# One fixed TensorE order for the attention of a two-layer hybrid block

## The chip, the cores and the metric

One core of a Trainium2 chip runs the whole program. The metric is device time in microseconds (us) of one execution, the median over runs. TensorE multiplies, VectorE (DVE), ScalarE (ACT) and GpSimd (POOL) do the elementwise work, and SyncE (SP) starts most DMAs.

## The reference

Two consecutive layers work on 512 latent tokens and 256 context tokens of width 1024. Layer 0 (a recurrent RWKV mixer with pooling, then a SwiGLU FFN) is not touched by the change. Layer 1 is neighbourhood attention over an 8 x 64 grid with 16 heads of 64, where every query also sees all 256 context keys in the same softmax, and then a SwiGLU FFN. The part that changes, cut to its core:

```python
q, k, v = split(h @ w_in, 3)                 # 512 latent tokens
kc, vc  = split(hc @ w_in[:, D:], 2)         # 256 context tokens
# each grid query looks at an 8 x 16 window, with a learned 2-D relative bias
s_loc = einsum('bqhd,bqnhd->bhqn', qr, kg) * scale + bias
s_ctx = einsum('bqhd,bnhd->bhqn', qr, kc) * scale
p = softmax(concatenate([s_loc, s_ctx], -1))
o = einsum('bhqn,bqnhd->bqhd', p[..., :n_loc], vg) + einsum('bhqn,bnhd->bqhd', p[..., n_loc:], vc)
out_lat = o.reshape(B, L, D) @ w_out
```

## The kernel before, in words

Activations lie with the 1024 features on partitions, as 8 slices of 128 features by 512 tokens. Every float32 product of activations with weights is made of three products of split operands (`mm3`, lines 115 to 121): high x high, high x low, low x high. A weight tile comes in by a DMA from the SP queue (`fetch`, lines 825 to 831), ACT casts its high part and DVE subtracts to get its low part.

Attention runs head pair by head pair: slice m of 8 holds heads 2m and 2m+1, one on partitions 0 to 63, the other on 64 to 127. For each m:

- `queries` (lines 644 to 658) makes the pair's q and k: two columns of 8 `mm3` each, so 2 x 24 matmuls of 512 columns, each column in a PSUM bank of tag `w` (two banks). After a column, ACT writes the high part (line 657 or 654) and DVE the low part (line 658 or 655).
- `attention` (lines 660 to 720) first loads the bias of both heads (4 DMAs from the SP queue, 6 POOL additions, line 675). Then it goes through 4 blocks `cb` of 128 queries. In each, for head j = 0 and then 1: six score matmuls of 256 columns with 64 rows (lines 686 and 687, recorded as lines 119 to 121) into a bank of tag `y` (three banks); the softmax (DVE lines 689, 693, 696; ACT line 695 with its accumulator read; POOL line 697); four transposes of 128 columns (line 700) into a bank of tag `v` (two banks) and ACT's copy of them (line 702). When both heads are there, 8 products with the values (line 711, recorded as 16 matmuls, the two heads on the two column halves) go to tag `s`, and every second block ACT copies them out (line 716, or 719 and 720 for the last pair).
- `mixed` (lines 722 to 728) casts the outputs of the first seven slices for the output projection `mixer_out` (8 columns of 8 `mm3`, 192 matmuls of 512 columns).

`latents` (lines 763 to 771) computes the values and the queries of pair 0, then for each m emits `attention(m)` together with `queries(m + 1)`, and for the last m with `mixed`. What order the engines run is not the order of emission: a planner takes, for each engine, among the instructions that its own model holds to be ready the one with the highest priority, which is the emission order here. So score, query, transpose and value matmuls of one or two pairs lie mixed on TensorE. `tc.issue_after(x)` is the one means to fix an order: what is emitted under it goes behind x in the queue of its engine.

Of the kernel before, what the change touches and what calls it, by code (L numbers as in the profile page):

```python
# [9 lines left out]
F32 = mybir.dt.float32  # L10
F32R = mybir.dt.float32r
AF = mybir.ActivationFunctionType
ALU = mybir.AluOpType
AX = mybir.AxisListType
PSUM = bass.MemoryType.PSUM

P = 128
# [12 lines left out]
CWR_, CWL_ = 3, 3  # L30
LATL, KEYL = 9, 0
REST = 1
POOL_S = 0
LEV = dict(c=1, C=2, p=0, s=0, q=1, m=4, a=5, l=5, L=5, X=2)

# [2 lines left out]
KD = 8  # L38
TL, TC = 512, 256
# [27 lines left out]
def chained(*gens):  # L67
    for g in gens:
        yield from g


class Kernel:
    def __init__(self, ctx, tc, a, out):
        self.ctx, self.tc, self.nc, self.a, self.out = ctx, tc, tc.nc, a, out
        self.now = 0
        self.ps = {}
        self.const = ctx.enter_context(tc.tile_pool(name="const", bufs=1))
        self.wp = ctx.enter_context(tc.tile_pool(name="wp", bufs=2))
# [36 lines left out]
    def mm3(self, ps, l, r, first, last, after=None):  # L115
        (lh, ll), (rh, rl) = l, r
        mm = self.nc.tensor.matmul
        with self.tc.issue_after(after.ins) if after else nullcontext():
            mm(ps, lhsT=lh, rhs=rh, start=first, stop=False)  # L119
        mm(ps, lhsT=lh, rhs=rl, start=False, stop=False)  # L120
        self.last = mm(ps, lhsT=ll, rhs=rh, start=False, stop=last)  # L121


    def setup(self):
# [519 lines left out]
    def queries(self, ap, f, m):  # L644

        nc, a = self.nc, self.a
        V = nc.vector
        new = lambda nm, n: [ap.tile([P, n], F32R, name=nm + s, tag=nm + s, bufs=2) for s in ("hi", "lo")]
        q, k = self.qk[m] = new("q", TL), new("k", TL)
        for j, src in enumerate((a.wq, a.wk)):  # L650
            ps = self.bank("w", (TL,))
            yield from f.column(ps, src[m], KD, f.act)
            if j:
                nc.scalar.copy(out=k[0], in_=ps)
                V.tensor_tensor(out=k[1], in0=ps, in1=k[0], op=ALU.subtract)
            else:
                nc.scalar.mul(out=q[0], in_=ps, mul=0.125)
                V.scalar_tensor_tensor(out=q[1], in0=ps, scalar=0.125, in1=q[0], op0=ALU.mult, op1=ALU.subtract)

    def attention(self, ap, f, m, o):  # L660
        nc, a = self.nc, self.a
        V, mm = nc.vector, nc.tensor.matmul
        v, vs = self.v
        (q, k), kc, vc = self.qk[m], self.kc[m], self.vc
        bm = []
        for j in range(2):

            run = ap.tile([P, 272], F32, name="run", tag="run", bufs=2)
            for hf in range(2):
                off = 16 + (2 * m + j) * 480 + 8 * hf  # L670
                src = bass.AP(a.rpb.tensor, a.rpb.offset + off, [[32, 8], [1, 8], [1, 272]])
                nc.sync.dma_start(out=run[64 * hf:64 * hf + 64, :], in_=src)
            b = ap.tile([P, 3, 256], F32, name="bm", tag="bm", bufs=3)
            for ty in range(3):
                nc.gpsimd.tensor_tensor(out=b[:, ty], in0=run[:, 8 * ty:8 * ty + 256], in1=self.mask[:, ty], op=ALU.add)
            bm.append(b)
        po = self.bank("s", (4, P))
        for cb in range(4):
            ty = (0, 1, 1, 2)[cb]
            gs = (0, 1, 3, 4)[cb]  # L680
            sT = [None] * 2
            for j in range(2):
                hd = slice(64 * j, 64 * j + 64)
                ps = self.bank("y")
                lq = tuple(x[hd, cb * P:cb * P + P] for x in q)
                self.mm3(ps[:, 0:256], lq, tuple(x[hd, 64 * gs:64 * gs + 256] for x in k), True, True)
                self.mm3(ps[:, 256:512], lq, tuple(x[hd, :] for x in kc), True, True)
                loc = ps[:, 0:256].rearrange("p (g r c) -> p g r c", g=4, r=8)
                V.tensor_tensor(
                    out=loc, in0=loc, in1=bm[j][:, ty, ::-1].rearrange("p (r g c) -> p g r c", g=4, r=8), op=ALU.add  # L690
                )
                mx = ap.tile([P, 2], F32, name="mx", tag="mx", bufs=4)
                V.tensor_reduce(out=mx[:, 0:1], in_=ps, axis=AX.X, op=ALU.max, negate=True)
                s = f.tmp("s")
                nc.scalar.activation(out=s, in_=ps, func=AF.Exp, bias=mx[:, 0:1], accum_out=mx[:, 1:2])
                V.reciprocal(out=mx[:, 1:2], in_=mx[:, 1:2])
                nc.gpsimd.tensor_scalar(out=s, in0=s, scalar1=mx[:, 1:2], scalar2=0.0, op0=ALU.mult, op1=ALU.add)
                pt = self.bank("v", (4, P))
                for i in range(4):
                    nc.tensor.transpose(out=pt[:, i, :], in_=s[:, i * P:i * P + P], identity=self.ident)  # L700
                sT[j] = f.tmp("sT", "ln").rearrange("p (i t) -> p i t", i=4)
                nc.scalar.copy(out=sT[j], in_=pt)
                yield 1
            for i in range(4):
                for j in range(2):
                    if i < 2:
                        src = v[:, gs // 2 + i] if gs % 2 == 0 else vs[:, gs // 2 + i]
                    else:
                        src = vc[:, i - 2]
                    hc = slice((2 * m + j) * 64, (2 * m + j) * 64 + 64)  # L710
                    mm(po[64 * j:64 * j + 64, cb, :], lhsT=src[:, hc], rhs=sT[j][:, i, :], start=i == 0, stop=i == 3)  # L711
            if cb % 2:
                cs = slice(P * cb - P, P * cb + P)
                done = po[:, cb - 1:cb + 1].rearrange("p c t -> p (c t)")
                if m < KD - 1:
                    nc.scalar.copy(out=o[:, m, cs], in_=done)
                else:
                    hi, lo = f.act(m)
                    nc.scalar.copy(out=hi[:, cs], in_=done)  # L719
                    V.tensor_tensor(out=lo[:, cs], in0=done, in1=hi[:, cs], op=ALU.subtract)  # L720

    def mixed(self, f, o):

# [6 lines left out]
    def latents(self, right):  # L730

        nc, a, tc, ctx = self.nc, self.a, self.tc, self.ctx
        self.turn = 0
        pool = lambda st, name, side="left": st.enter_context(tc.tile_pool(name=name, bufs=1, side=side))
        kv = pool(ctx, "kv")
        psl = self.psum("psl", "y")
        self.banks["y"] = 3
        ctx.enter_context(psl)
        f = Flow(self, pool(ctx, "lp"), "l", TC, TL, 0, "ywywy", LBG, dict(t=3, ln=4, f=2, whi=3, wlo=3))
        f.load()  # L740
        f.mix()
        run = lambda g: [None for _ in g]
        with self.level(LATL):
            run(f.mixer_out(0, a.w_out, MIX))
        with ExitStack() as st:
            gp = pool(st, "gp")
            new = lambda: gp.tile([P, 512], F32, name="aw", tag="aw", bufs=NAW_)
            md = lambda: gp.tile([P, 512], F32, name="md", tag="aw", bufs=NAW_)
            self.emit((LATL, f.ffn(0, gp, 4, 5), 528), (LATL, self.adas([(1, g) for g in range(12)], lambda: self.bank("v"), new, NAW_, md), 150))
            last = self.last  # L750
            self.join_norm(1)
            self.join_norm(2)
            with self.level(KEYL):
                run(self.context_keys(kv, last))
            run(f.normed(1))
        right.close()
        with ExitStack() as st:
            ap = pool(st, "ap")
            self.mask = ap.tile([P, 3, 256], F32, name="mask")
            nc.scalar.dma_start(out=self.mask, in_=a.mask)  # L760
            self.qk = [None] * KD
            o = ap.tile([P, KD, TL], F32, name="o")
            run(self.values(ap, f))
            run(self.queries(ap, f, 0))
            for m in range(KD):
                parts = [(0, self.attention(ap, f, m, o), 8)]
                if m + 1 < KD:
                    parts.append((0, self.queries(ap, f, m + 1), 16))
                else:
                    parts.append((0, self.mixed(f, o), 7))  # L770
                self.emit(*parts)
        run(f.mixer_out(2, a.w_out1))
        run(f.ffn(1, pool(ctx, "gp1"), 11, 16))
        run(f.normed(3, True))
# [666 lines left out]
```

## Time and profile before

| | before |
|---|---|
| median of 3 runs | 2420.7 us (2420.57 to 2421.53) |
| profiled execution, device time | 2430.38 us |
| its span, first to last instruction | 2428.6 us |
| TensorE busy | 2212.5 us (91%) |
| VectorE busy | 1220.3 us (50%) |
| ScalarE busy | 996.7 us (41%) |
| GpSimd busy | 659.6 us (27%) |

The profile is one execution, recorded on the chip. A row of the timeline gives the start of an instruction, how long it took, its engine, its source line, the operation, and "out<-in" with the program's tile names. Matmuls overlap: the distance between the starts of two neighbours is what a matmul costs TensorE, not its own duration. All `mm3` matmuls bear lines 119 to 121; in the attention those with 64 rows are scores, those with tiles `lhhi`, `lhlo`, `whi`, `wlo` are the projections.

### The profile page before, as it was taken

How to read it: one execution, taken by the hardware profiler on the slowest of the kernel's cores; microseconds unless marked ns; L12 is line 12 of the kernel's file. 1: busy time of each engine (PE TensorE's matmuls, PEld its weight loads, DVE VectorE, ACT ScalarE, POOL GpSimd, SP SyncE). 2: the span in 40 equal slices, each digit the busy share in tenths (PEclk: the TensorE clock that was granted, in tenths of full speed). 3: DMA queues.
4: the chain of work that ended last, by engine and by line, in shares of the span. 5: the costliest groups of instructions: out<-in, count | busy, mean ns of one | idle time of the engine just before them, and what ended most of it. 6: DMA issues, size and time to landing. Idle time of an engine off the chain costs nothing.

```text
span 2428.6 us, 44519 instructions
## 1 busy us (share of the span) xinstructions
PE 2212.5 (91%) x16944; PEld 1760.6 (72%) x16944; DVE 1220.3 (50%) x2529; ACT 996.7 (41%) x2075; POOL 659.6 (27%) x643
## 2 busy tenths in 40 slices
PE   7888888889879898979999999998999998999995
PEld 4776666656657777758788877877777776888874
DVE  2756555636656764225633553357454465333343
ACT  3545334444534643334533332234354544322332
POOL 2431202121322432556732300023133342000021
PEclk9888889879978899989999999999999998999997
DMA  7765466566843454575544335323511112333332
GB/s 268 230 181 176 116 193 185 169 173 183 235 125 91 137 141 121 160 252 185 174 127 130 115 124 165 99 83 113 144 45 49 43 52 66 96 95 97 96 90 66
DMA packets 324678, 327.35 MB, mean 135 GB/s; under 512 B 137328, under 2 KB 214768, under 8 KB 324464
## 3 DMA queue, kind: packets, MB, share of 16 engines
q1 hardware_dynamic: 320720, 317.45, 44.1%
q10 hardware_dynamic: 2592, 3.90, 0.5%
q8 instruction: 133, 2.18, 0.4%
q0 software_dynamic: 1152, 3.15, 0.3%
q14 instruction: 81, 0.66, 0.1%
HBM read 280.02 MB, written 42.80 MB: 133 GB/s over the span
## 4 chain that ended last, share of the span: by engine, by line
PE 62%; DVE 6%; DMA 5%; ACT 2%; issue 1%; SPq 1%; POOL 0%; POOLq 0%; DVEq 0%; ACTq 0%
PE y L119 8%; PE y L120 7%; PE y L121 7%; PE w L119 6%; PE w L121 6%; PE w L120 6%; PE s L119 3%; PE s L120 3%; PE s L121 3%; PE s L711 2%; PE v L700 1%; PE v L195 1%; PE w L1099 1%; DVE n L879 1%; DVE pr L1133 1%
## 5 line engine op out<-in xcount | busy, mean ns | idle before, releaser
L829 ACT CAST whi<-wraw 128x512 fp32r<-128x512 f32 (+2 forms) x560 | 329.3, 593 | 697.8 <-PE y L120 261.1
L830 DVE TENSOR_TENSOR wlo<-wraw,whi 128x512 fp32r<-128x512 f32 (+2 forms) x384 | 285.7, 747 | 357.2 <-ACT whi L829 330.3
L830 POOL TENSOR_TENSOR wlo<-wraw,whi 128x512 fp32r<-128x512 f32 (+2 forms) x176 | 202.4, 1157 | 297.2 <-ACT whi L829 269.7
L107 POOL TENSOR_TENSOR wlo<-wraw,whi 128x512 fp32r<-128x512 f32 x92 | 121.5, 1322 | 290.0 <-ACT whi L106 260.8
L119 PE MATMUL w<-lhhi,whi 128*128 128x512 f32 x472 | 189.2, 402 | 9.9 <-ACT lhhi L954 5.3
L119 PE MATMUL y<-lhhi,whi 128*128 128x512 f32 x488 | 192.3, 394 | 0.5 <-ACT lhhi L719 0.5
L121 PE MATMUL y<-lhhi,wlo 128*128 128x512 f32 x488 | 190.5, 391 | 0.0
L120 PE MATMUL y<-lhlo,whi 128*128 128x512 f32 x488 | 190.5, 390 | 0.0
L120 PE MATMUL w<-lhlo,whi 128*128 128x512 f32 x472 | 188.1, 399 | 1.8 <-DVE lhlo L879 1.5
L121 PE MATMUL w<-lhhi,wlo 128*128 128x512 f32 x472 | 187.4, 397 | 0.1
L855 POOL TENSOR_TENSOR lxz<-lxz,s 128x512 f32<-128x512 f32 x28 | 43.3, 1579 | 510.3 <-ACT s L861 510.3
L119 PE MATMUL s<-chhi,whi 128*128 128x256 f32 x480 | 144.5, 301 | 23.0 <-DVE kclo L610 9.3
L119 PE MATMUL g<-hhi,whi 128*128 128x256 f32 (+1 forms) x368 | 140.4, 381 | 14.2 <-DVE nr L480 5.4
L121 PE MATMUL s<-chhi,wlo 128*128 128x256 f32 x480 | 142.4, 297 | 0.4 <-POOL wlo L830 0.4
L120 PE MATMUL s<-chlo,whi 128*128 128x256 f32 x480 | 142.8, 297 | 0.0
L121 PE MATMUL g<-hhi,wlo 128*128 128x256 f32 (+1 forms) x368 | 137.1, 373 | 2.0 <-POOL wlo L107 1.8
L120 PE MATMUL g<-hlo,whi 128*128 128x256 f32 (+1 forms) x368 | 134.1, 364 | 0.0
L119 PEld LDWEIGHTS s<-chhi,whi 128*128 128x128 f32 x480 | 96.5, 201 | 31.4 <-DVE kclo L610 9.7
L119 PEld LDWEIGHTS w<-lhhi,whi 128*128 128x128 f32 x472 | 89.1, 189 | 33.6 <-ACT lhhi L926 7.5
L119 PEld LDWEIGHTS y<-lhhi,whi 128*128 128x128 f32 x488 | 91.9, 188 | 21.9 <-issue 3.0
L120 PEld LDWEIGHTS w<-lhlo,whi 128*128 128x128 f32 x472 | 89.4, 189 | 25.3 <-DVE lhlo L879 4.9
L121 PEld LDWEIGHTS y<-lhhi,wlo 128*128 128x128 f32 x488 | 91.8, 188 | 19.6 <-DVE n L879 0.8
(360 smaller groups left out, 5138.6 us busy)
## 6 DMA issues: line engine op xcount, KB each, us to landing
wraw<-w SPq DMA_DIRECT2D x368, 256.0 KB
aw<-ada_w SPq DMA_DIRECT2D x128, 256.0 KB
wraw<-w_in SPq DMA_DIRECT2D x92, 256.0 KB
bk<-bk SPq DMA_DIRECT2D x72, 256.0 KB
wraw<-ada_w SPq DMA_DIRECT2D x64, 256.0 KB
wraw<-w_out SPq DMA_DIRECT2D x48, 256.0 KB
wraw<-wk SPq DMA_DIRECT2D x32, 256.0 KB
wraw<-wv SPq DMA_DIRECT2D x32, 256.0 KB
```

Source lines behind the costliest of these rows:

```text
L107: (self.nc.gpsimd if POOL_LO else self.nc.vector).tensor_tensor(out=lo, in0=raw, in1=hi, op=ALU.subtract)
L119: mm(ps, lhsT=lh, rhs=rh, start=first, stop=False)
L120: mm(ps, lhsT=lh, rhs=rl, start=False, stop=False)
L121: self.last = mm(ps, lhsT=ll, rhs=rh, start=False, stop=last)
L195: mm = nc.tensor.matmul(ps[32 * q:32 * q + 32, part], lhsT=self.cs[:, k + q, :], rhs=w[q // step][:, q % step, :], start=k == 0, stop=k > ...
L700: nc.tensor.transpose(out=pt[:, i, :], in_=s[:, i * P:i * P + P], identity=self.ident)
L711: mm(po[64 * j:64 * j + 64, cb, :], lhsT=src[:, hc], rhs=sT[j][:, i, :], start=i == 0, stop=i == 3)
L829: self.nc.scalar.copy(out=hi, in_=raw)
L830: self.lo.tensor_tensor(out=lo, in0=raw, in1=hi, op=ALU.subtract)
L855: tt = lambda o, x, y, op, e=V: e.tensor_tensor(out=o, in0=x, in1=y, op=op)
L879: tt = lambda o, x, y, op, e=V: e.tensor_tensor(out=o, in0=x, in1=y, op=op)
L1099: nc.tensor.matmul(ps[w][hd[h ^ w], c, :], lhsT=bk[hd[h], w, c, :], rhs=LH[0][hd[h], c, :], start=True, stop=True,)
```

## The change

The attention of all 8 pairs becomes one pipeline of 32 steps (m, cb). Every TensorE instruction in it is put behind the one before it with `issue_after` (the handle `self.tail`), so TensorE's order is the emission order:

- First the scores of step 0 and then 8 `mm3` of the later queries (`ALEAD`), which is the q column of pair 1.
- Then for each i: the scores of step i+1, four `mm3` of the later queries as long as there are any, the eight transposes of step i (both heads), and the value products of step i-1. There are 7 x 16 = 112 later `mm3`, 8 ahead and 4 in each of the 26 following iterations, so the last six steps have none.
- The scores of both heads alternate: for each of the six products the one of head 0 (rows 0 to 63) and then that of head 1 (rows 64 to 127), into two different banks. The four score banks are three of tag `y` and one of tag `w`. All later query columns share the one `w` bank that is left (`self.wide`); before, they had two.
- The bias of pair m+1 is loaded at step 4m; its tile has 4 buffers instead of 3. The probabilities have a tag of their own with 6 buffers.
- `mixed` is emitted two slices at a time in the last four iterations. The chain ends (`self.tail = None`) ahead of the output projection.

The arithmetic is the same. The diff, cut to its core:

```diff
     def mm3(self, ps, l, r, first, last, after=None):
+        after = after or self.tail
         with self.tc.issue_after(after.ins) if after else nullcontext():
             mm(ps, lhsT=lh, rhs=rh, start=first, stop=False)
         mm(ps, lhsT=lh, rhs=rl, start=False, stop=False)
         self.last = mm(ps, lhsT=ll, rhs=rh, start=False, stop=last)
+        if self.tail:
+            self.tail = self.last
...
     def queries(self, ap, f, m):
-            ps = self.bank("w", (TL,))
+            ps = self.bank("w", (TL,)) if self.wide is None else self.wide
             yield from f.column(ps, src[m], KD, f.act)
...
+    def block(self, calls):
+        for c in calls:
+            with self.tc.issue_after(self.tail.ins):
+                self.tail = c()
+
+    def probabilities(self, ap, m, cb):
...
+        banks = self.pairs[cb % 2]
+        def score(j, c, i):
+            hd = slice(64 * j, 64 * j + 64)
+            r, cs = (kc, slice(0, TC)) if c else (k, slice(64 * gs, 64 * gs + 256))
+            return lambda: mm(
+                banks[j][:, 256 * c:256 * c + 256], lhsT=q[i == 2][hd, cb * P:cb * P + P], rhs=r[i == 1][hd, cs], start=i == 0, stop=i == 2
+            )
+        self.block([score(j, c, i) for c in range(2) for i in range(3) for j in (0, 1)])
+        for j in range(2):
...                       (bias, maximum, Exp, reciprocal, scaling: the same six instructions as before)
+    def turned(self, f, m, cb):
+        pt = [self.bank("v", (4, P)) for _ in range(2)]
+        self.block([turn(j, i) for j in (1, 0) for i in range(4)])
+        for j in (1, 0):
+            out.insert(0, f.tmp("sT", "ln").rearrange("p (i t) -> p i t", i=4))
+            nc.scalar.copy(out=out[0], in_=pt[j])
+
+    def weighted(self, f, m, cb, o):
+        self.block([part(i, j) for i in range(4) for j in range(2)])
...                       (copy out after every second block, as before)
+    def attention(self, ap, f, o):
+        self.po = self.bank("s", (2, 2, P))
+        self.pairs = [self.bank("y"), self.bank("y")], [self.bank("y"), self.bank("w")]
+        self.wide = self.bank("w")
+        steps = [(m, cb) for m in range(KD) for cb in range(4)]
+        later, mixed = chained(*(self.queries(ap, f, m) for m in range(1, KD))), self.mixed(f, o)
+        more = lambda n: [None for _ in islice(later, n)]
+        self.biases(ap, 0)
+        self.tail = self.last
+        self.probabilities(ap, *steps[0])
+        more(ALEAD)
+        for i in range(len(steps) + 1):
+            if i < len(steps) and steps[i][1] == 0 and steps[i][0] < KD - 1:
+                self.biases(ap, steps[i][0] + 1)
+            if i + 1 < len(steps):
+                self.probabilities(ap, *steps[i + 1])
+            more(4)
+            if i < len(steps):
+                self.turned(f, *steps[i])
+            if i:
+                self.weighted(f, *steps[i - 1], o)
+            if i > 4 * KD - 4:
+                list(islice(mixed, 2))
+        more(99)
+        self.tail = None
+        list(mixed)
```

## Rows read from the trace of the kernel before

**Rows 1.** The page, section 1: busy time, share of the span, instructions.

```profile
PE 2212.5 (91%) x16944; PEld 1760.6 (72%) x16944; DVE 1220.3 (50%) x2529; ACT 996.7 (41%) x2075; POOL 659.6 (27%) x643
```

**Rows 2.** Busy time in stretches: length, engines with instruction counts, clock, DMA share.

```profile
1755.90:1940.00 184.10, 184.10 (x1232) 137.24 (x1232) 94.36 (x204) 95.64 (x215) 64.06 (x89) 1.00 0.16 46
...
1739.50:2013.80 274.30, 273.08 (x1731) 206.96 (x1730) 143.37 (x280) 133.46 (x290) 95.31 (x116) 1.00 0.20 58
```

**Rows 3.** Groups by line and shape, TensorE, 1739.5 to 2013.8 us.

```profile
L119 PE MATMUL w<-lhhi,whi 128*128 128x512 f32 x152 | 62.6, 412 | 0.0
...
L119 PE MATMUL y<-lhhi,whi 128*128 128x512 f32 x40 | 16.2, 405 | 0.5 <-ACT lhhi L719 0.5
```

**Rows 4.** Timeline of TensorE, the query products of pair 0 and after.

```profile
1739.77 0.39 PE L120 MATMUL w<-lhlo,whi 128*128 128x512 f32 x1
...
1755.63 0.39 PE L121 MATMUL w<-lhhi,wlo 128*128 128x512 f32 x1
```

**Rows 5.** Timeline of TensorE: scores of two heads side by side, then query products.

```profile
1955.46 0.39 PE L119 MATMUL y<-kchi,qhi 64*128 64x256 f32 x1
...
1955.69 0.28 PE L120 MATMUL y<-kclo,qhi 64*128 64x256 f32 x1
...
1955.81 0.27 PE L121 MATMUL y<-kchi,qlo 64*128 64x256 f32 x1
1955.82 0.28 PE L119 MATMUL y<-kchi,qhi 64*128 64x256 f32 x1
...
1956.05 0.27 PE L121 MATMUL y<-kchi,qlo 64*128 64x256 f32 x1
1956.26 0.50 PE L119 MATMUL w<-lhhi,whi 128*128 128x512 f32 x1
1956.59 0.39 PE L120 MATMUL w<-lhlo,whi 128*128 128x512 f32 x1
```

**Rows 6.** Timeline of TensorE: the six scores of one head alone.

```profile
1965.36 0.38 PE L119 MATMUL y<-khi,qhi 64*128 64x256 f32 x1
...
1966.07 0.28 PE L121 MATMUL y<-kchi,qlo 64*128 64x256 f32 x1
```

**Rows 7.** Timeline of TensorE: transposes and value products in whole blocks.

```profile
1947.54 0.39 PE L121 MATMUL w<-lhhi,wlo 128*128 128x512 f32 x1
1947.77 0.60 PE L700 MATMUL v<-cst,s 128*128 128x128 f32 x4
1948.30 0.66 PE L711 MATMUL s<-sT,vs 128*64 128x128 f32 x8
...
1949.33 0.66 PE L700 MATMUL v<-cst,s 128*128 128x128 f32 x4
...
1971.46 1.09 PE L700 MATMUL v<-cst,s 128*128 128x128 f32 x8
1972.31 0.47 PE L121 MATMUL y<-lhhi,wlo 128*128 128x512 f32 x1
```

**Rows 8.** Timeline of all engines: the softmax of one head, after its last score.

```profile
1966.38 0.43 DVE L689 TENSOR_TENSOR y<-y,bm 128x256 f32<-128x256 f32 x1 [1.22 <-PE y L121]
...
1966.92 0.69 DVE L693 TENSOR_REDUCE mx<-y 128x1 f32<-128x512 f32 x1
...
1968.68 0.17 DVE L696 RECIPROCAL mx<-mx 128x1 f32<-128x1 f32 x1 [1.00 <-ACT s L695]
...
1969.02 0.70 POOL L697 TENSOR_SCALAR s<-s,mx 128x512 f32<-128x512 f32 x1 [0.47 <-DVE mx L696]
```

**Rows 9.** Timeline: end of the k column of pair 0, its two evictions.

```profile
1750.19 0.39 PE L121 MATMUL w<-lhhi,wlo 128*128 128x512 f32 x1
...
1751.66 0.68 DVE L655 TENSOR_TENSOR klo<-w,khi 128x512 fp32r<-128x512 f32 x1
```

**Rows 10.** Timeline: a later q column's last product, its evictions.

```profile
1899.19 0.40 PE L121 MATMUL w<-lhhi,wlo 128*128 128x512 f32 x1
...
1901.42 0.68 DVE L658 SCALAR_TENSOR_TENSOR qlo<-w,qhi 128x512 fp32r<-128x512 f32 x1
```

More of the change, by code (lines that the diff above doesn't have):

```diff
@@ L32 @@
 REST = 1
+ALEAD = 8
 POOL_S = 0
@@ L658, in queries, with biases @@
                 V.scalar_tensor_tensor(out=q[1], in0=ps, scalar=0.125, in1=q[0], op0=ALU.mult, op1=ALU.subtract)
-    def attention(self, ap, f, m, o):
+    def biases(self, ap, m):
         nc, a = self.nc, self.a
[L662 to L665, printed above, removed]
+        bm = self.bm[m] = []
         for j in range(2):
@@ L672, in attention @@
                 nc.sync.dma_start(out=run[64 * hf:64 * hf + 64, :], in_=src)
-            b = ap.tile([P, 3, 256], F32, name="bm", tag="bm", bufs=3)
+            b = ap.tile([P, 3, 256], F32, name="bm", tag="bm", bufs=4)
             for ty in range(3):
@@ L676, in attention @@
             bm.append(b)
[L677 to L720, printed above, removed]
@@ new lines, in block @@
+    def block(self, calls):
[3 more added lines that the diff above has]
+    def probabilities(self, ap, m, cb):
+        nc = self.nc
+        V, mm = nc.vector, nc.tensor.matmul
+        (q, k), kc, bm = self.qk[m], self.kc[m], self.bm[m]
+        ty, gs = (0, 1, 1, 2)[cb], (0, 1, 3, 4)[cb]
+        banks = self.pairs[cb % 2]
[6 more added lines that the diff above has]
+        self.block([score(j, c, i) for c in range(2) for i in range(3) for j in (0, 1)])
+        out = []
+        for j in range(2):
+            ps = banks[j]
+            loc = ps[:, 0:256].rearrange("p (g r c) -> p g r c", g=4, r=8)
+            V.tensor_tensor(
+                out=loc, in0=loc, in1=bm[j][:, ty, ::-1].rearrange("p (r g c) -> p g r c", g=4, r=8), op=ALU.add
+            )
+            mx = ap.tile([P, 2], F32, name="mx", tag="mx", bufs=6)
+            V.tensor_reduce(out=mx[:, 0:1], in_=ps, axis=AX.X, op=ALU.max, negate=True)
+            s = ap.tile([P, 512], F32, name="s", tag="s", bufs=6)
+            nc.scalar.activation(out=s, in_=ps, func=AF.Exp, bias=mx[:, 0:1], accum_out=mx[:, 1:2])
+            V.reciprocal(out=mx[:, 1:2], in_=mx[:, 1:2])
+            nc.gpsimd.tensor_scalar(out=s, in0=s, scalar1=mx[:, 1:2], scalar2=0.0, op0=ALU.mult, op1=ALU.add)
+            out.append(s)
+        self.probs[m, cb] = out
@@ new lines, in turned @@
+    def turned(self, f, m, cb):
+        nc = self.nc
+        s = self.probs.pop((m, cb))
+        pt = [self.bank("v", (4, P)) for _ in range(2)]
+        turn = lambda j, i: lambda: nc.tensor.transpose(out=pt[j][:, i, :], in_=s[j][:, i * P:i * P + P], identity=self.ident)
+        self.block([turn(j, i) for j in (1, 0) for i in range(4)])
+        out = self.sT[m, cb] = []
+        for j in (1, 0):
+            out.insert(0, f.tmp("sT", "ln").rearrange("p (i t) -> p i t", i=4))
+            nc.scalar.copy(out=out[0], in_=pt[j])
@@ new lines, in weighted, with part @@
+    def weighted(self, f, m, cb, o):
+        nc = self.nc
+        V, mm = nc.vector, nc.tensor.matmul
+        v, vs = self.v
+        sT, gs = self.sT.pop((m, cb)), (0, 1, 3, 4)[cb]
+        po = self.po[:, cb // 2, cb % 2]
+        def part(i, j):
+            src = self.vc[:, i - 2] if i > 1 else (vs if gs % 2 else v)[:, gs // 2 + i]
+            hc = slice((2 * m + j) * 64, (2 * m + j) * 64 + 64)
+            return lambda: mm(po[64 * j:64 * j + 64, :], lhsT=src[:, hc], rhs=sT[j][:, i, :], start=i == 0, stop=i == 3)
+        self.block([part(i, j) for i in range(4) for j in range(2)])
+        if cb % 2:
+            cs = slice(P * cb - P, P * cb + P)
+            done = self.po[:, cb // 2].rearrange("p c t -> p (c t)")
+            if m < KD - 1:
+                nc.scalar.copy(out=o[:, m, cs], in_=done)
+            else:
+                hi, lo = f.act(m)
+                nc.scalar.copy(out=hi[:, cs], in_=done)
+                V.tensor_tensor(out=lo[:, cs], in0=done, in1=hi[:, cs], op=ALU.subtract)
@@ new lines, in attention @@
+    def attention(self, ap, f, o):
+        self.bm, self.probs, self.sT = {}, {}, {}
+        self.po = self.bank("s", (2, 2, P))
[21 more added lines that the diff above has]
+        more(99)
+        self.tail = None
+        list(mixed)
@@ L760, in latents @@
             nc.scalar.dma_start(out=self.mask, in_=a.mask)
-            self.qk = [None] * KD
+            self.qk, self.wide = [None] * KD, None
             o = ap.tile([P, KD, TL], F32, name="o")
@@ L764, in latents @@
             run(self.queries(ap, f, 0))
[L765 to L771, printed above, removed]
+            self.attention(ap, f, o)
         run(f.mixer_out(2, a.w_out1))
```

## The prediction

> **What bounds the kernel now.** I read the page's section 1 first: TensorE is busy 91% of the span, the next engine half of it [rows 1]. Then the stretches: in the attention (1755.9 to 1940) TensorE is busy for all of the 184.1 us while VectorE and ScalarE have about half to spare, the clock is granted in full (1.00, the 2.4 GHz level) and the DMA engines are 16% busy [rows 2]. So here only what TensorE itself spends counts, and the reader is to see in the timeline how it spends it. The stretch that the change can touch runs from the first query product of pair 0 to the last product of the output projection, 1739.5 to 2013.8, 274.3 us [rows 2]. In it stand 152 + 40 = 192 triples of 512-column products [rows 3], so 576 matmuls: 48 for pair 0's q and k, 336 for the other pairs, 192 for the output projection. Undisturbed they come 0.227 us apart (70 intervals in 15.86 us) [rows 4], 130.5 us in all. The other 143.8 us are scores, transposes, value products and what the mixing costs. That is the sum to beat.
>
> **Unit costs, read from places where the old order happens to do what the new one always does.**
> - Scores, both heads alternating. The two matmuls of a pair start 0.01 us apart, and pairs follow at 0.12; the first gap after a change of shape is 0.23, the way out to a query product 0.21 [rows 5]. Six pairs: 0.23 + 4 x 0.12 + 0.21 = 0.92 us a step. One head alone needs five gaps of together 0.71 and the same way out [rows 6], so two heads one after the other 1.8.
> - Four query steps, 12 matmuls: the first gap after scores is 0.33, 0.10 more than the next ones at 0.23 [rows 5]; the way to a transpose costs nothing extra, being a gap like the others. 0.33 + 11 x 0.23 = 2.86.
> - Eight transposes: four and the way out to the values take 0.53, and eight take 0.85 together, so four more at 0.11 [rows 7]: 0.97. After scores, where the shape changes, 0.05 more.
> - Sixteen value matmuls with the way out: 1948.30 to 1949.33, 1.03 [rows 7].
>
> **The sum.** Scores 32 x 0.92 = 29.4. Queries 26 x 2.86 = 74.4, and the 24 ahead of the loop 5.7 (with one shape change at each end). Transposes 26 x 0.97 + 6 x 1.02 = 31.3. Values 32 x 1.03 = 33.0. Together 173.8. Pair 0's queries 48 x 0.227 = 10.9 and the output projection 192 x 0.227 = 43.5 stay. Without a wait that is 228.2, 46 less than 274.3. The gain is not the score pairing alone (some 0.9 x 32 = 28 if nothing had been paired; less, as the old order pairs some by chance): the rest is fewer changes of shape, each 0.1 at either side, since the new order has three a step.
>
> **The waits that the new order adds.** All of TensorE's attention is one queue, so behind a waiting matmul everything of the stage waits.
> 1. Start. The scores of step 0 need pair 0's k, low part too. The last k product starts at 1750.19, the low part is done at 1752.34, 2.15 later [rows 9]; with 0.23 of it the product itself, TensorE stands 2.0 us. Before, the next pair's q column ran over this.
> 2. The one bank for query columns. A column must be evicted by ScalarE, then VectorE before the next begins. After pair 1's q column only the scores of step 1 lie between: 2.15 - 0.33 - 0.92 leaves about 1.0. Later, a column ends every second step, and transposes, values and scores lie between: 0.23 + 0.97 + 1.03 + 0.92 = 3.15 us. The k eviction needs 2.15; a late one, behind a softmax and a weight cast on ScalarE, 2.91 (1899.19 to 1902.10) [rows 10]. I take zero for these 13 boundaries; one more ScalarE operation in front (0.7) would cost 0.5 each, 6 us.
> 3. Softmax. From the last score of one head to its scaled probabilities pass 3.65 us (1966.07 [rows 6] to 1969.72 [rows 8]); the second head's addition and maximum (0.54 + 0.69) come behind the first's, so 4.9. In the steps with queries, 2.86 + 0.97 + 1.03 + 0.92 + 2.86 lie between scores and their transposes, 8.6: hidden, with 3.7 to spare. In the last steps without queries, 0.2 + 1.02 + 1.03 + 0.92 = 3.2: every other step stands 1.7 (the wait of one step is the next one's cover), two in all, and step 31, with no scores left in between, 2.6. Together 6.0. Output-projection matmuls are outside the chain and may be planned into these gaps, as the old order did; `mixed` readies their inputs only in the last four iterations, so I give back 2.
> 4. Bias and weights. The bias loads move one pair ahead of their use on SP's queue, and the POOL additions (mean of POOL's instructions 64.06/89 = 0.72 us) with them; three of them in front of a scaling delay it by 2.2, under the 3.7 to spare. If that cover went, it would be some 2 us at each of 7 pairs. Weight loads come one per step of 5.8 us with the DMA engines at 16% [rows 2]: nothing. The four banks for scores, the transposes' two and the probabilities' six tiles are free a step or more ahead: nothing.
> 5. What the sum does not hold (the projection's first sum, its last cast, small lateness of ScalarE and VectorE, whose 133.5 and 143.4 us in the whole stretch [rows 2] are at most 4.2 and 4.5 a step of 5.8): 5 us, a choice, between 2 and 18.
>
> 228.2 + 2.0 + 1.0 + 6.0 - 2.0 + 5.0 = 240.2, so 34 us less. The profiled execution took 2430.4 (span 2428.6 and 1.8 around it), the median 2420.7, 0.4% lower; 34 scaled is still 34: about 2386 us.
>
> **A rule that speaks against it.** Pairs follow at 0.12 us with both heads' weight loads in that time [rows 5]. The Trainium skill (TensorE: Matmul & The Clock Gate, Part 3, "The mechanism") says that a weight load overlaps a running matmul only if it goes to another row group. By it the next load for a half would wait for that half's matmul; with the page's 128 columns at 1.2 GHz, 0.107 us a load, a pair would take an estimated 0.21, scores 1.4 a step, and the time would be about 2401. This trace disagrees as far as it goes.
>
> **Rivals.**
> - Steady waits eat half. ScalarE works in order, and its order is fixed by the planner's model; if evictions and copies come late by 0.5 us a step, 32 x 0.5 = 16 are lost: about 2403. For it: the margin of 0.2 us in the late eviction [rows 10]. Against: all other margins are over 3 us.
> - The pairs do not run side by side (the rule above, or runs that are only short by chance): 10 gaps of 0.12, then 0.22 + 1.2 + 0.21 = 1.63 a step, 0.7 x 32 = 23 more: 2409. Against: three pairs in a row here [rows 5].
> - Slower. The eviction of a query column is emitted only when the next query step is asked for, behind the next step's softmax. If the planner keeps that order on ScalarE and VectorE, the next column waits from the next step's scores on: 4.9 less the scaling (1.1) for both heads' Exp, then the eviction, 2.15 less the 0.39 of the product [rows 9], less the way out, 0.2: about 5.4 a boundary, 13 x 5.4 = 70. That decides from 34/13 = 2.6 us a boundary on; the time would be 2386 + 70 = 2456. For it: the emission order. Against: before, evictions are emitted the same way, and these two are done 2.15 and 2.91 us after the start of their last product [rows 9, 10].
> - The change does not do what it says: the old order may already be as good as the chain. The 143.8 against 97.5 (scores, transposes, values and lead-in shape changes, 173.8 less 336 x 0.227) speaks against it: 2420.
>
> **How the numbers follow.** A measurement here can tell about 0.2%, 4.8 us. Forecast (gain 25 to 43) 0.70; steady waits (10 to 25) 0.14; pairs not side by side 0.04; no effect 0.04; eviction order 0.05; another loss (a planner's order gone wrong in later stages) 0.03. Faster 0.88, same 0.04, slower 0.08. The low end is the sum with no unpriced waits and gaps filled, 274.3 - 230 = 44: 2376. The high end takes in most of the steady waits: 2406.
>
> **What would show it.** In the profile after: scores in pairs 0.12 apart, about 0.9 a step; a step with queries every 5.8 us and 26 of them in 150 us; one wait of about 2 us at the start, one of 1 before pair 1's k, three of about 2 at the end. Wrong would be a step much over 6 us, TensorE waiting for line 657 or 658 or for the copies of the transposes, or single gaps of 0.2 between pairs.

## The result, and the profile after

The changed kernel takes 2383.0 us (median of 4 runs, 2378.3 to 2388.6) against 2420.6 (4 runs, 2414.9 to 2421.5) for the kernel before. The ratio is 0.9849, 95% interval 0.9825 to 0.9872: 31 to 42 us less. 2386 was forecast, within 2376 to 2406.

Section 1 of the page after, to be read against [rows 1]: no engine has other work, but TensorE is busy for 49.4 us less with the same 16944 matmuls.

```profile
PE 2163.1 (91%) x16944; PEld 1735.9 (73%) x16944; DVE 1226.7 (52%) x2529; ACT 994.5 (42%) x2075; POOL 660.5 (28%) x643
```

Busy time in stretches of the kernel after (length, engines with instruction counts, clock, DMA share, GB/s): the stage from pair 0's first query product to the output projection's last product, and 24 steps with queries in it.

```profile
1731.20:1964.40 233.20, 229.48 (x1731) 187.30 (x1729) 144.62 (x280) 130.03 (x290) 93.62 (x113) 1.00 0.23 69
1762.00:1899.90 137.90, 137.90 (x1154) 113.47 (x1152) 88.96 (x186) 84.26 (x198) 60.47 (x84) 1.00 0.19 57
```

The same 1731 matmuls that took 274.3 us [rows 2] now take 233.2, and the 24 steps have not one idle moment on TensorE: 137.9 / 24 = 5.75 us each. One such step, TensorE's timeline of the kernel after:

```profile
1762.03 0.38 PE L700 MATMUL y<-khi,qhi 64*128 64x256 f32 x1
1762.03 0.38 PE L700 MATMUL w<-khi,qhi 64*128 64x256 f32 x1
...
1762.60 0.28 PE L700 MATMUL y<-kclo,qhi 64*128 64x256 f32 x1
1762.60 0.28 PE L700 MATMUL w<-kclo,qhi 64*128 64x256 f32 x1
1762.72 0.27 PE L700 MATMUL y<-kchi,qlo 64*128 64x256 f32 x1
1762.72 0.28 PE L700 MATMUL w<-kchi,qlo 64*128 64x256 f32 x1
1762.93 0.50 PE L123 MATMUL w<-lhhi,whi 128*128 128x512 f32 x1
...
1765.56 0.39 PE L125 MATMUL w<-lhhi,wlo 128*128 128x512 f32 x1
1765.79 1.03 PE L725 MATMUL v<-cst,s 128*128 128x128 f32 x8
1766.75 0.66 PE L743 MATMUL s<-sT,vs 128*64 128x128 f32 x8
...
1767.77 0.39 PE L700 MATMUL y<-khi,qhi 64*128 64x256 f32 x2
```

Bank y is head 0, bank w head 1: the two of a pair start within 0.01 us, pairs are 0.12 apart. Scores with the way out take 0.90 (1762.03 to 1762.93), twelve query products 2.86, transposes 0.96, values 1.02. All parts were read in the old order's lucky places [rows 5, 7].

The profiled executions differ by 49.1 us in their spans. Of this 41.1 lies in the stage. 8.35 is an earlier start of it, in a part where both kernels run the same instructions, but for a handful in the same order; before's profiled execution was itself 9.7 above its median. After the stage both take 415 us. The medians' 37.7 agree with a stage of 41 within their interval. So below kernels are compared by this stage, and by the interval of their times. Here it is for every kernel, with the number of runs of one kind (scores, transposes, values, 512-column products) on TensorE, and the number of score pairs, of 192 (384 score matmuls), whose second matmul starts within 0.06 us of the first:

| kernel | stage, us | runs | side by side | step in the middle, us |
|---|---|---|---|---|
| before | 274.2 | 247 | 52 | |
| after; again | 233.1; 233.3 | 131 | 192 | 5.75 |
| e1_unpaired | 247.5 | 132 | 96 | 6.09 |
| e2_free | 235.9 | 162 | 176 | |
| e3_nolook | 326.0 | 129 | 192 | 7.0, every fourth 11.0 to 11.3 |
| e4_order | 244.5 | 132 | 192 | 5.94 |
| e5_mid | 266.8 | 133 | 192 | 5.75 and 7.85 |
| e6_before_paired | 255.1 | 191 | 173 | |
| e7_double | 235.0 | 111 | 191 | 5.5 to 5.6 |
| e8_start | 234.2 | 129 | 192 | 5.79 |
| e9_double2 | 228.7 | 109 | 192 | 5.5 |

Where the 41 us come from can be summed from the timelines. What a matmul costs is the distance to the next one's start; here these distances are added up over the stage's 1728 matmuls of the four kinds, by whether the two are of one kind or of two (a change of kind, with any wait that stands there):

| us between starts | scores | values | transposes | 512-column | changes of kind | sum |
|---|---|---|---|---|---|---|
| before | 37.5 | 31.4 | 24.2 | 125.3 | 55.6 | 274.0 |
| e6_before_paired | 22.6 | 32.0 | 25.3 | 127.6 | 47.4 | 254.8 |
| after | 23.1 | 26.3 | 24.4 | 128.9 | 30.2 | 232.9 |

From before to after 14 us go between scores and 25 at changes of kind; 4 of these come back between 512-column products, as there are now more such neighbours. The other 5 are a pairing that the prediction does not count: the value products of the two heads start side by side too (within 0.06 us), 198 of 256 pairs before and all 256 after.

### The profile page after: what moved, and what is told of

Its sections match the earlier page's. It is cut to its first block, busy times and chain, and to the rows that moved or that the text cites. A ratio compares the mean times of both kernels' runs of the same rounds, so it can differ in the third digit from the quotient of the medians.

```text
span 2379.5 us, 44426 instructions
## 1 busy us (share of the span) xinstructions
PE 2163.1 (91%) x16944; PEld 1735.9 (73%) x16944; DVE 1226.7 (52%) x2529; ACT 994.5 (42%) x2075; POOL 660.5 (28%) x643
## 4 chain that ended last, share of the span: by engine, by line
PE 62%; DVE 6%; DMA 5%; issue 2%; ACT 2%; SPq 1%; POOL 1%; POOLq 0%; ACTq 0%; DVEq 0%
PE y L123 7%; PE y L125 7%; PE y L124 7%; PE w L123 6%; PE w L124 6%; PE w L125 6%; PE s L123 3%; PE s L125 3%; PE s L124 3%; PE s L743 1%; PE w L1157 1%; DMA wraw<-w 1%; PE v L201 1%; PE v L725 1%; PE y L700 1%
## 5 line engine op out<-in xcount | busy, mean ns | idle before, releaser
L888 DVE TENSOR_TENSOR wlo<-wraw,whi 128x512 fp32r<-128x512 f32 (+2 forms) x384 | 293.1, 767 | 339.6 <-ACT whi L887 316.1
L123 PE MATMUL w<-lhhi,whi 128*128 128x512 f32 x472 | 189.3, 403 | 11.3 <-ACT lhhi L1012 5.8
L110 POOL TENSOR_TENSOR wlo<-wraw,whi 128x512 fp32r<-128x512 f32 x92 | 121.4, 1323 | 280.1 <-ACT whi L109 233.3
```

The costliest lines, as they stand in the source:

```text
L110: (self.nc.gpsimd if POOL_LO else self.nc.vector).tensor_tensor(out=lo, in0=raw, in1=hi, op=ALU.subtract)
L888: self.lo.tensor_tensor(out=lo, in0=raw, in1=hi, op=ALU.subtract)
```

## The experiments

**Both heads' scores, one head after the other (e1_unpaired).** The chain stays; head 1's six products follow head 0's.

```diff
-self.block([score(j, c, i) for c in range(2) for i in range(3) for j in (0, 1)])
+self.block([score(j, c, i) for j in (0, 1) for c in range(2) for i in range(3)])
```

> The changed kernel with one edit: the twelve scores of a step go head by head (six of head 0, then six of head 1) instead of alternating. Theory (two matmuls on the two row halves run side by side, so alternating saves the pair's second one): scores of a step take 0.22 + 10 x 0.12 + 0.21 = 1.6 us instead of 0.91, a step with queries 6.45 instead of 5.75, 0.7 x 32 = 22 us more: about 2405. Rival (the gain is all from the fixed order and fewer changes of shape, the pairs cost the same either way): steps stay at 5.75, 2383.

Measured: 2394.1 us (8 runs), ratio 0.9912 (0.988 to 0.9944), so 11 us above the kernel after by the medians (15 by the ratios); a step takes 6.09. The direction is the theory's, the price half of it. TensorE's timeline of one step says why:

```profile
1803.98 0.38 PE L700 MATMUL y<-khi,qhi 64*128 64x256 f32 x1
...
1804.32 0.28 PE L700 MATMUL y<-khi,qlo 64*128 64x256 f32 x1
1804.33 0.39 PE L700 MATMUL w<-khi,qhi 64*128 64x256 f32 x1
...
1804.55 0.28 PE L700 MATMUL w<-klo,qhi 64*128 64x256 f32 x1
1804.55 0.28 PE L700 MATMUL y<-kclo,qhi 64*128 64x256 f32 x1
...
1805.02 0.28 PE L700 MATMUL w<-kchi,qlo 64*128 64x256 f32 x1
```

Head 1's first product, emitted as the seventh, starts 0.01 us after head 0's third. Three of six pairs form without being asked for. The pairing's price is 0.34 x 32 = 11 us, not 22. (The stage's other 3 us lie at the start, behind a later load, below.)

**No chain (e2_free).** The emission order, the banks and the look-ahead stay; the planner may place what it wants.

```diff
-        after = after or self.tail
...
-            with self.tc.issue_after(self.tail.ins):
-                self.tail = c()
+            self.tail = c()
```

> The changed kernel with the same emission, banks and buffers, but without the chain: no matmul of the attention is put behind another, so the planner orders TensorE freely. Theory (the chain itself is needed, since the planner mixes scores, transposes, values and queries into short runs and pairs scores only by chance): more than 150 runs of one kind against about 130, and between half and all of the 41 us of the stage lost, 2403 to 2424. Rival (the emission order, the four score banks and the look-ahead do it, the planner would keep that order by its priorities): within 5 us of 2383.

Measured: 2378.6 us (4 runs), ratio 0.9858 (0.9825 to 0.9891), stage 235.9. The theory that the fixed order makes the gain falls; the rival holds. A stretch of its TensorE timeline shows the planner's freedom: two score products of the next step slip in before the transposes, and query products come between these; but the runs stay long, mostly twelve query products and sixteen values.

```profile
1799.00 0.66 PE L741 MATMUL s<-sT,v 128*64 128x128 f32 x8
...
1800.02 0.38 PE L698 MATMUL y<-khi,qhi 64*128 64x256 f32 x1
...
1800.83 0.29 PE L698 MATMUL y<-khi,qhi 64*128 64x256 f32 x2
1801.05 0.66 PE L723 MATMUL v<-cst,s 128*128 128x128 f32 x4
1801.46 0.47 PE L122 MATMUL w<-lhhi,whi 128*128 128x512 f32 x1
```

The chain buys some 3 us of stage (4 in the 24 steps from the transposes of step 4 to those of step 28, counted from 0: 138.1 us against 134.0), and the times don't resolve even that. Which part of the rest does it, the emission order, the four score banks or the larger buffers, was not run apart; that the look-ahead is needed shows in e3_nolook.

**Pairing alone, in the kernel before (e6_before_paired).** In the old block the two heads' scores are emitted alternating, chained among themselves; softmax, transposes and values stay.

```diff
+banks = [self.bank("y") for _ in range(2)]
...
+            for j in range(2):
...
+                with self.tc.issue_after(prev.ins) if prev else nullcontext():
+                    prev = mm(banks[j][...], lhsT=q[i == 2][...], rhs=r[i == 1][...], ...)
```

> The kernel before with one part of the change: in each block of 128 queries the twelve scores of both heads are emitted alternating and kept in that order, everything else as it was and left to the planner. Theory (in the new order pairing is worth 14 us of the stage, the rest comes from fewer changes of shape on TensorE): pairs rise from 52 to nearly 192, 140 x 0.118 = 17 us, and both heads' scores in one run instead of two take some changes of shape with them, up to 8: stage 250 to 258 us of 274, about 2396 to 2404. Rival (the pairs are all that counts): the whole 41 us of the stage, 2380. Other rival (the planner's order spoils what pairing gives): no faster than 2415.

Measured: 2404.2 us (7 runs), ratio 0.9929 (0.9903 to 0.9955), stage 255.1: pairing brings 19 of the 41 us. It is not pairing alone: the scores of both heads now stand in longer runs, so that 56 changes of kind go with it (247 to 191), and the table of distances has 15 us less between scores and 8 less at changes, with 4 more elsewhere. What it leaves stands in TensorE's timeline: the grain is still a few matmuls, and the values wait for a copy between two of theirs.

```profile
1798.90 0.38 PE L690 MATMUL y<-khi,qhi 64*128 64x256 f32 x1
1799.36 0.66 PE L708 MATMUL v<-cst,s 128*128 128x128 f32 x4
1799.95 0.43 PE L719 MATMUL s<-sT,vs 128*64 128x128 f32 x2
1800.75 0.54 PE L719 MATMUL s<-sT,vs 128*64 128x128 f32 x5 [0.37 <-ACT sT L710]
```

**One more change of kind a step (e4_order).** Values of step i-1 ahead of the transposes of step i.

```diff
-            if i < len(steps): self.turned(...)
-            if i: self.weighted(...)
+            if i: self.weighted(...)
+            if i < len(steps): self.turned(...)
```

> The changed kernel with the values of step i-1 ahead of the transposes of step i, so that TensorE goes scores, queries, values, transposes: four changes of shape a step with queries instead of three (queries and transposes have the same shape and no longer touch). Theory (a change of shape costs 0.09 on the way out and 0.05 to 0.1 on the way in): a step of 5.75 us becomes 5.90, the stage 4 us longer. Rival (what counts is only how often a block ends, not its shape): 5.75.

Measured: one run, 2397.2 us. The step is 5.94 us from one first score to the next, in its timeline:

```profile
1801.57 0.39 PE L700 MATMUL y<-khi,qhi 64*128 64x256 f32 x2
...
1806.48 1.09 PE L725 MATMUL v<-cst,s 128*128 128x128 f32 x8
1807.51 0.38 PE L700 MATMUL y<-khi,qhi 64*128 64x256 f32 x1
```

0.19 us more than after: query products to transposes share a shape, and here the values stand between. So one more change costs about what the theory said (0.15). This price does not carry the rest of the gain. From before to after 247 - 131 = 116 changes go, but 56 of them went with pairing already; the 22 us of stage that e6_before_paired leaves go with the other 60, 11 us at 0.19 each. The table of distances says what the 22 are: 17 at changes of kind, where e6_before_paired also has waits (values up to 0.57 behind transposes, where 0.20 is the plain distance), and 6 between values (216 of 256 pairs side by side there, and some waits as in its rows above), less 1 that comes back elsewhere. Of the stage's 11.4 us above after, 5 are the step; most others are a later start.

**No look-ahead (e3_nolook).** A step's scores are issued in its own iteration, before the four query steps and its transposes.

```diff
-            if i + 1 < len(steps):
-                self.probabilities(ap, *steps[i + 1])
+            if 0 < i < len(steps):
+                self.probabilities(ap, *steps[i])
```

> The changed kernel without the look-ahead of one step: the scores of step i, then its four query steps, then its own transposes, then the values of step i-1, still in one chain. Theory (a softmax of both heads takes 4.9 us from the last score, of which only 0.2 + 2.9 are covered now): TensorE stands 1.8 us in each of 26 steps, 47 us, and 4.7 in each of the six without queries less what the output projection fills, 10 to 28: about 2440 to 2458, so slower than the kernel before. Rival (softmax is short enough, and the look-ahead buys nothing): steps stay at 5.75, under 2390.

Measured: 2467.4 us (4 runs), ratio 1.0224 (1.0189 to 1.026): slower than the kernel before, by more than expected. The regular step is 7.0 us, with 1.43 instead of 0.23 from the last query product to the transposes. Every fourth one is worse, as this timeline of all engines shows (the last column is the idle time before and what ended it):

```profile
1799.10 3.92 POOL L679 TENSOR_TENSOR bm<-run,mask 128x256 f32<-128x256 f32 x5
...
1800.43 0.39 PE L125 MATMUL w<-lhhi,wlo 128*128 128x512 f32 x1
...
1800.85 0.16 DVE L715 RECIPROCAL mx<-mx 128x1 f32<-128x1 f32 x1 [0.50 <-ACT s L714]
...
1803.00 1.36 POOL L716 TENSOR_SCALAR s<-s,mx 128x512 f32<-128x512 f32 x2
...
1804.41 0.47 PE L725 MATMUL v<-cst,s 128*128 128x128 f32 x1 [3.60 <-POOL s L716]
```

The scaling's input is ready at 1801.0, but POOL adds five biases until 1803.0. That is the 2 us that the prediction priced for the bias "if that cover went". And then the clock: the stretch behind this wait, from the view of stretches.

```profile
1804.40:1808.60 4.20, 4.19 (x27) 3.53 (x29) 0.00 (x0) 1.17 (x2) 0.00 (x0) 0.50 0.18 47
```

After the 4 us without a matmul the granted clock was 0.50, the lower of the two levels (1.2 GHz), over these 4.2 us; transposes, values and scores took 5.4 us from 1804.4 on, where a step of the kernel after has 2.9 for them.

**The column boundary moved into the middle of a block (e5_mid).** Ten query steps ahead of the loop, so that every second block holds the last product of one column and the first of the next.

```diff
-ALEAD = 8
+ALEAD = 10
```

> The changed kernel with ten query steps ahead of the loop instead of eight, so that every query column ends in the middle of four query steps and nothing lies between it and the next column, which uses the same bank. Theory (the eviction of a column, 2.15 us from the start of its last product, is hidden only because transposes, values and scores lie between two columns): about 2.0 us at each of 13 boundaries, 26 less the 0.9 that the first one costs already, so 25 us more: 2408. Rival (evictions are never the limit): 2383.

Measured: 2409.9 us (10 runs), ratio 0.9984 (0.9954 to 1.0013): the change's gain is gone. TensorE's timeline at one boundary:

```profile
1774.32 0.39 PE L125 MATMUL w<-lhhi,wlo 128*128 128x512 f32 x1
1776.52 0.50 PE L123 MATMUL w<-lhhi,whi 128*128 128x512 f32 x1 [1.81 <-DVE qlo L664]
```

2.20 instead of 0.23, at each of 13 boundaries: 26 us, less the 1.0 that the first one costs in the kernel after too, so 25 as expected; the medians differ by 27. One bank for the columns is enough only because the three other blocks lie over its eviction. The stage is 33.7 us longer, some 9 more than that, most of it at the start. In four chained kernels (e1, e3, e4, e5) the first scores come 14.4 to 15.1 us after the first query product, in the kernel after and its repeat 12.0 and 12.3. Timeline of all engines of e5_mid:

```profile
1738.23 1.24 ACT L887 CAST whi<-wraw 128x512 fp32r<-128x512 f32 x2 [6.58 <-DMA wraw<-wq]
...
1739.37 0.58 ACT L660 CAST khi<-w 128x512 fp32r<-128x512 f32 x1
...
1740.01 0.39 PE L700 MATMUL y<-khi,qhi 64*128 64x256 f32 x2 [4.00 <-ACT khi L660]
```

and the 4 us from there in the view of stretches:

```profile
1740.00:1744.00 4.00, 3.54 (x16) 2.81 (x17) 2.40 (x6) 0.19 (x1) 0.00 (x0) 0.59 0.39 131
```

The eviction of k stands behind two casts of the next column's weights on ScalarE, and these wait for a load. TensorE idles 4.0 us, and the clock falls. Whether these kernels or only these executions have the later load stays open: by their medians e1 and e5 lie 11 and 27 us above after, near the loop's price alone (11 and 25), by their ratios 15 and 33, the whole stage's (14 and 34).

**The first query column ahead of the first scores (e8_start).**

```diff
-        self.probabilities(ap, *steps[0])
         more(ALEAD)
+        self.probabilities(ap, *steps[0])
```

> The changed kernel with one edit: the q column of pair 1 stands ahead of the scores of step 0 instead of behind them. Theory (the wait at the start is for pair 0's k, evicted on ScalarE behind casts of weights that a DMA brings late; with a column of 24 matmuls ahead it is hidden, whatever the DMA does): 16.4 us from the first query product to the first score without a gap, then 7 to 8 to the first transpose, together 23.5 to 24.5 in place of 24.1 (26 to 29 where the DMA was late); stage 232 to 234 and no half clock. Rival (the wait only moves behind the scores, to the column that needs the one bank, and to the transposes): 26 or more together.

Measured: 2378.3 us (5 runs), ratio 0.9831 (0.9807 to 0.9854), stage 234.2. The wait for k is gone, but the first transposes now have only twelve query products over their softmax:

```profile
1744.23 0.39 PE L125 MATMUL w<-lhhi,wlo 128*128 128x512 f32 x1
1747.62 1.09 PE L725 MATMUL v<-cst,s 128*128 128x128 f32 x8 [2.99 <-POOL s L716]
```

From the first query product to the first transposes it is 24.3 us, within the theory's 23.5 to 24.5 and no less than the 24.1 of the kernel after: the wait has moved. The clock stays at 1.00 behind it (1747.62 to 1752.00). That this order does not depend on the load is an argument only: the one profiled execution has no late load.

**Two steps together (e7_double, e9_double2), beside the kernel after again (after_again).** Scores of two steps at once, query products 6 + 9 + 9 around two blocks of transposes, then both steps' values; evictions emitted at the column's end. e9 issues the second column between the first scores and the loop.

```diff
...
+            if i + 2 < len(steps):
+                self.probabilities(ap, *steps[i + 2])
+                self.probabilities(ap, *steps[i + 3])
+            more(2)
+            self.turned(f, *steps[i])
+            more(3)
+            self.turned(f, *steps[i + 1])
+            more(3)
+            self.weighted(f, *steps[i], o)
+            self.weighted(f, *steps[i + 1], o)
...
```

> A further version: the changed kernel with two steps taken together (scores of two steps, two query steps, transposes, three query steps, transposes, three query steps, values of two steps), so three changes of shape for two steps instead of six, the q column of pair 1 ahead of the first scores, and a column's evictions emitted right behind its last product. Theory: 10.93 us for two steps instead of 11.50, 13 x 0.57 = 7.4, and 2 at the start: stage 224, about 2374. Rival (something else, softmax or evictions, becomes the bound as the scores of two steps come at once): steps of two above 11.5 with visible waits, no faster than 2383.

> The changed kernel itself on the same chip as the further version, for a comparison in the same runs: ratio to the kernel before 0.985, stage 233 us.

> The further version mended: two steps taken together, and now the q column of pair 1 ahead of the first scores and its k column behind the scores of steps 0 and 1, so that nothing follows directly on scores whose softmax it needs. Theory: the 4.5 us wait at the start and the half clock behind it go (12 us of start instead of 29), two steps with queries in 11.0 us throughout; the four pairs of steps without queries are bound by VectorE (some 5.8 us each): stage about 227, 6 to 10 us below the changed kernel, ratio to the kernel before 0.981 to 0.983. Rival (the steps without queries, now eight instead of six, eat what the shape changes give): 0.985 or more.

Measured: e7 2378.2 us (6 runs), ratio 0.9838 (0.9803 to 0.9874), stage 235.0; after again 2385.3 (6 runs), 0.9852 (0.9821 to 0.9883), 233.3; e9 2375.7 (6 runs), 0.9829 (0.9805 to 0.9854), 228.7. In e7 the loop's gain is lost at the start: steps 0 to 3 have their scores back to back, the second two wait 4.55 us for the first two's banks, and run at the lower clock. e9 fills that hole. Its TensorE timeline, one round of two steps:

```profile
1780.78 0.39 PE L703 MATMUL y<-khi,qhi 64*128 64x256 f32 x2
...
1789.88 0.66 PE L746 MATMUL s<-sT,vs 128*64 128x128 f32 x8
...
1791.78 0.39 PE L703 MATMUL y<-khi,qhi 64*128 64x256 f32 x2
```

11.00 us for two steps instead of 11.50. Its stage is the shortest, 4.5 us under after, and its ratio agrees with the expectation (0.981 to 0.983). But 4.5 us is 0.19% of the time, and the intervals of the two kernels overlap: shown in the stage, not in the time.

## Why the prediction was right

The mechanism and most of the sizes held; two terms were too large. The stage was predicted at 240.2 us and took 233.1. That the forecast median is only 3 us off is in part luck: the stage was missed by 7, and the medians moved 3 less than the stage of the profiled executions. (The low end's 230 should have been 231 by its own terms; nothing hangs on it.)

- **Pure work.** 228.2 from parts, 5.78 a step; the step measured 5.75. Parts of a loop that does not exist yet can be summed, if the old order does each of them whole somewhere.
- **The rule on weight loads.** All 192 score pairs run side by side, at 0.12 a pair: a step's scores took 0.90. The overlap limit of the Trainium skill (TensorE: Matmul & The Clock Gate, Part 3, "The mechanism"), by which they would have taken an estimated 1.4, is not seen.
- **Start.** 2.0 predicted. The low part of k is used 2.20 us after k's last product started; less the product (0.23) and the first score pair, which runs meanwhile (0.23), TensorE lost 1.7. All engines, kernel after:

```profile
1741.42 1.25 ACT L887 CAST whi<-wraw 128x512 fp32r<-128x512 f32 x2 [3.70 <-DMA wraw<-wq]
...
1741.84 0.39 PE L125 MATMUL w<-lhhi,wlo 128*128 128x512 f32 x1
...
1742.57 0.58 ACT L660 CAST khi<-w 128x512 fp32r<-128x512 f32 x1
...
1743.20 0.39 PE L700 MATMUL y<-khi,qhi 64*128 64x256 f32 x2 [0.97 <-ACT khi L660]
...
1744.04 0.38 PE L700 MATMUL y<-klo,qhi 64*128 64x256 f32 x2 [0.46 <-DVE klo L661]
```

  The casts ahead of the k eviction and their wait for a load were not in the prediction. Here they end just in time; in e5_mid they cost 2 us more, and the clock.
- **Pair 1's boundary.** 1.0 predicted; 1.23 less the way out of 0.21, 1.0, between these rows of TensorE's timeline of the kernel after:

```profile
1751.18 0.27 PE L700 MATMUL w<-kchi,qlo 64*128 64x256 f32 x1
1752.41 0.50 PE L123 MATMUL w<-lhhi,whi 128*128 128x512 f32 x1 [0.95 <-DVE qlo L664]
```

- **The later boundaries.** There are 12; the prediction's 13 count pair 1's among them. No wait was predicted and none is there: no idle time in the 24 steps. The slower rival (70 us) needed the evictions behind the softmax, and they are not. But the margin is real: without cover a boundary costs 2.0 (e5_mid).
- **Tail and the unpriced rest.** 6.0 less 2.0, and 5.0: together 9.0. Measured, 233.1 - 228.2 - 1.7 - 1.0 = 2.2. This is the mis-sized term. The projection fills the tail far better than the 2 us given back. At its first step without queries the transposes come only 0.39 after the scores (0.21 is the plain way out), and after four of them ten projection products lie where the wait was expected. TensorE's timeline of the kernel after:

```profile
1900.64 0.28 PE L700 MATMUL w<-kchi,qlo 64*128 64x256 f32 x1
1901.03 0.66 PE L725 MATMUL v<-cst,s 128*128 128x128 f32 x4
1901.44 0.47 PE L123 MATMUL w<-lhhi,whi 128*128 128x512 f32 x1
```

  The later steps have 2, 6, 0 and 24 products there, and one wait of 0.44. The rest are the projection's first sum, half a microsecond behind the last values, and a break of 1.5 in the projection for two foreign products (`lxz`); both are there before too. Steps that are 0.03 shorter than summed give 0.8 back.
- **Steady waits** (0.5 a step in the rival): none, with ScalarE at 84.3 and VectorE at 89.0 of 137.9 us.
- **Where the argument was too narrow.** The prediction gave pairs and grouping as the gain, and the distances show both: 14 us between scores, 21 at changes of kind less what comes back between 512-column products. The 5 between values it did not name. It priced the loss of pairing at 0.7 a step and it is 0.34, and it spoke of the chain as what orders TensorE. Without the chain the planner comes within 3 us of its stage.

## What to carry to other kernels

Where one engine is busy all the time, add up the distances between its starts by kind, and count its changes of kind and the matmuls that could run side by side: these 41 us came from both, with not one instruction removed. A price per change from one experiment is not to be multiplied by all changes saved, as some of them went with another part of the gain. Issue the next step's first part before this step's last, so that a softmax or an eviction always has whole blocks of other work over it, and let the emission order say it before a hard chain does. Ahead of the loop look at what stands in front of the first eviction on its engine: there a late load costs its wait and then the clock.

## What the runs showed of the hardware that was not expected

- The row halves of TensorE are not in step: a score product of head 1 started 0.01 us after head 0's third, though it was emitted behind head 0's sixth (e1_unpaired). Half of the pairing comes without alternating.
- After a wait of about 4 us the granted clock was 0.50 to 0.59 for the next 4 us (e3_nolook, e5_mid), so a wait there cost some 2 us on top of itself (5.4 less 2.9 in e3_nolook). In the kernel after, which waited 1.36 and 0.84 between matmuls at its start, it stayed at 1.00 from 1743.2 to 1747.0.
